# Modulation products in plain float32 on four column strips of the array

## Chip, cores and metric

The kernel runs on one core of a Trainium2 chip. The metric is the device time of one execution in microseconds (us). PE is the tensor engine, DVE the vector engine, ACT the scalar engine, POOL GpSimd and SP the queue that issues most DMAs.

## What is computed

Two layers of a diffusion block on 256 latent and 256 context tokens of width 1024. Each layer begins with a modulation: the conditioning vectors `c` (latent) and `c_ctx` (context) pass a SiLU and are multiplied with a 1024 x 6144 matrix.

```python
s_c, s_cc = silu(c), silu(c_ctx)
mod   = s_c  @ w_ada[l] + b_ada[l]      # 6144 numbers: sh1, sc1, g1, sh2, sc2, g2
mod_c = s_cc @ w_ada[l] + b_ada[l]
y  = mixer_sublayer(x * (1 + sc1) + sh1, ...)       # conv | attention | Hyena | SSD, then w_out
x  = layer_norm(alpha * x + g1 * y)
x  = layer_norm(alpha * x + g2 * peer(x * (1 + sc2) + sh2, ...))   # expert layer, 16384 experts
```

All weights are float32. The result is the latent stream after two layers.

## The kernel before

The modulation is cut into 12 chunks of 512 columns per layer, `c4` = 0 to 11; chunks 0 and 1 are sh1, 2 and 3 sc1, 4 and 5 g1, 6 to 9 sh2 and sc2, 10 and 11 g2. `ada_steps(l, c4, use)` makes one chunk from four loads of `w_ada` of 512 KB each (two halves `j` of 256 columns, two halves `q` of the 1024 rows), here called tiles. A tile holds four blocks of 128 rows, `k` = 0 to 3. The two SiLU vectors are the stationary operand (128 rows, 2 or 4 columns), the weights move through. All eight row blocks of a half accumulate into the same two or four rows of a PSUM bank `pm`.

There are two ways for the product. Where `prep` has a "split" entry, the tile is cut into two `float32r` numbers: ACT casts it to `w_hi` (L140), DVE or POOL subtracts to get `w_lo` (L141), and two products per block (L275, L276) multiply both with `s4`, which holds the vector's own high and low part. Fourteen chunks go that way: the first four of layer 0, five during the expert layer's query stage of layer 0, five in layer 1's mixers. Ten chunks go without: one plain float32 product per block (L278). A plain float32 product leaves two records in the trace, a `float32r` one leaves one.

The finished rows are copied by ACT to `rw` (L284) and then turned into columns. For the first four chunks `to_cols_pe` does it with four small float32 products against a selection matrix (`pt`, L298), the bias being a fifth row. For other chunks below 10 `to_cols` writes the rows to DRAM (`ad`, L303), reads them back element by element, one DMA for each row (`ct`, L307), and DVE adds the bias (L310) and, after a split, the low part (L312). Chunks 10 and 11 are spread with `row_out` (`pg`, L317) and stored as rows.

The program has a start (the first four chunks, then the modulated input `h`, split into `hT`), the mixers' projections (`pj`), a stretch in which the generators `ssd()`, `attention()`, `hyena()`, `conf_norm()` and `more()` take turns, the output projection (`po`), the query stage of the expert layer (`pq`, `ss`, top-k on DVE), the expert tables (`G`, `au`, `ov`), and the same again for layer 1. `more()` and, in the query stage, a call after each query block draw chunks one tile at a time from `modulations()`. A list scheduler orders each engine's instructions by program order and a simulated timeline; the engines run their queues in order. Tiles of `w_ada` are held in rings: six buffers at the start, three (`fwp`) for the rest of layer 0, the four of `w_raw` in layer 1, which the projections use too. A load waits until its ring has a free buffer.

Of the kernel before, what the change touches and what calls it, by code (L numbers as in the profile page):

```python
# [10 lines left out]
F32 = mybir.dt.float32  # L11
F32R = mybir.dt.float32r
# [4 lines left out]
ALU = mybir.AluOpType  # L17
# [21 lines left out]
WRB = (3, 4)  # L39
WLB = (2, 3)  # L40
# [5 lines left out]
WHB = (4, 5)  # L46
FP = ((), (4, 5, 6))
WB = 3
# [6 lines left out]
GRB = (3, 2)  # L55
def AE(G, V): return (G,)
UEV = (0, 0)
AEV = 2
GB = 8
# [27 lines left out]
def tile_hybrid_diffusion(ctx: ExitStack, tc: tile.TileContext, I: dict, out: bass.AP):  # L87
    nc = tc.nc
# [30 lines left out]
    cp = pool("cp")  # L119
# [32 lines left out]
    sT = mk(cp, [128, 8, 2], name="sT")  # L152
    s4 = mk(cp, [128, 8, 4], F32R, name="s4")
    cnt, wdma = [0], [None]
# [98 lines left out]

    def ada_steps(l, c4, use, pe_bias=False):

        pm = bank("pm")
        pr, nb = prep["raw"]
        sp = prep.get("split")
        if sp and c4 in FP[l] and not pe_bias:
            sp = None  # L260
        nr = 4 if sp else 2
        for j in range(2):
            o = pm[0:nr, j * 256:(j + 1) * 256]
            for q in range(2):
                raw = mk(pr, [128, 8, 128], tag=prep.get("tag", "wa_raw"), bufs=nb).rearrange("p (k a) c -> p k (a c)", a=2)
                wdma[0] = nc.sync.dma_start(raw, I["w_ada"][l, 2 * c4 + j, q])
                if sp:
                    hi, lo = (mk(sp[0], [128, 8, 128], F32R, tag=t, bufs=sp[1]) for t in ("w_hi", "w_lo"))
                    hi, lo = (a.rearrange("p (k a) c -> p k (a c)", a=2) for a in (hi, lo))
                    cnt[0] += 1  # L270
                    split(raw, hi, lo, sp[2][cnt[0] % len(sp[2])])
                for k in range(4):
                    st, sp_ = q == 0 and k == 0, q == 1 and k == 3
# [8 lines left out]
        if pe_bias or c4 >= 10:  # L282
            nc.sync.dma_start(rw[nr:nr + 1, :], I["b_ada"][l, c4:c4 + 1, :])
        S.copy(rw[0:nr, :], pm[0:nr, :])  # L284
        use(rw, nr)
        yield
# [7 lines left out]

    def to_cols_pe(rw, nr, l, m0, c):
        pt = bank("pt")
        for j in range(4):
            T.matmul(pt[:, 128 * j:128 * j + 128], rw[0:5, j * 128:(j + 1) * 128], sel[0:5, 0:128], start=True, stop=True)  # L298
        V.tensor_scalar(modTs[l][:, m0:m0 + 4, :], pt.rearrange("p (a b) -> p a b", b=128)[:, :, 0:2], 1.0 if c in SCL else 0.0, None, op0=ALU.add)

    def to_cols(rw, nr, l, m0, c):
        ad = mk(dr, [nr, 512], tag=f"ad{nr}", bufs=2)
        nc.sync.dma_start(ad, rw[0:nr, :])  # L303
        ct = mk(lnp, [128, 4, nr], tag=f"ct{nr}")
        with nc.allow_non_contiguous_dma(reason="a few columns"):
            for r in range(nr):
                nc.sync.dma_start(ct[:, :, r], ad[r].rearrange("(m p) -> p m", p=128))  # L307
        o = modTs[l][:, m0:m0 + 4, :]
        bias = bTs[l][:, 4 * c:4 * c + 4, None].to_broadcast([128, 4, 2])
        V.tensor_tensor(o, ct[:, :, 0:2], bias, ALU.add)  # L310
        if nr == 4:
            V.tensor_tensor(o, o, ct[:, :, 2:4], ALU.add)  # L312

    def row_out(rw, nr, dst, s):
        pg = bank("pg")
        c = (384 if nr == 2 else 128) + s * 128
        T.matmul(pg, sel[0:nr + 1, c:c + 128], rw[0:nr + 1, :], start=True, stop=True)  # L317
        ro = mk(lnp, [1, 512], tag="ro1")
        S.copy(ro, pg[0:1, :])
        nc.sync.dma_start(dst, ro)  # L320
# [517 lines left out]
    MC = {0: 0, 1: 4, 2: 8, 3: 12, 4: 16, 5: 20, 6: 24, 7: 28, 8: 32, 9: 36}  # L838
    SCL = (2, 3, 8, 9)
    g2d = mk(dr, [3, D], name="g2d")  # L840
    xd = mk(dr, [4, 128, D], name="xd")
    prep = {}
    done = [(0, 3)]

    def modulations():

        def g2row(rw, nr, rows, c):
            for s, r in rows:
                row_out(rw, nr, g2d[r:r + 1, (c % 2) * 512:(c % 2) * 512 + 512], s)
        for l, c in [(0, c) for c in range(4, 12)] + [(1, c) for c in range(12)]:  # L850
            def use(rw, nr):
                if c < 10:
                    to_cols(rw, nr, l, MC[c], c)
                else:
                    g2row(rw, nr, ((0, 0), (1, 1)) if l == 0 else ((0, 2),), c)
                done.append((l, c))
            for _ in ada_steps(l, c, use):
                yield (l, c)
# [15 lines left out]
    for l in range(2):  # L874
# [11 lines left out]
        with ExitStack() as mx:  # L886
# [15 lines left out]
            else:  # L902
                with ExitStack() as hs_:
                    hmp = pool("hmp", bufs=2, stack=hs_)
                    prep.update(raw=(hmp, 6), split=(hmp, 3, (V, G)))
                    xt = yT
                    fs_ = pool("fs", stack=fl_s, side="right")

                    def early():
                        nc.sync.dma_start(sel, I["sel"])  # L910
                        nc.sync.dma_start(cm, I["cm"])
                        yield
                        for j in range(2):
                            nc.sync.dma_start(sms[j], I["sm"][j])
                            nc.gpsimd.dma_start(rowss[j], I["rows"][j].partition_broadcast(128))
                        nc.sync.dma_start(dfts[0], I["dft"][:, 0:2])
                        for j in range(2):
                            for _ in hyena_filter(j, fs_, fs_, dfts[0]):
                                yield
                    side = early()  # L920

                    def first():
                        pend = []
                        for i, c4 in enumerate((0, 2, 1, 3)):
                            late = pend
                            pend = []
                            for _ in ada_steps(0, c4, lambda rw, nr: pend.append((rw, nr, 0, MC[c4], c4)), True):
                                for a in late:
                                    to_cols_pe(*a)
                                late = []  # L930
                                yield
                        to_cols_pe(*pend[0])
                    for i, _ in enumerate(first()):
# [14 lines left out]
                prep.update(raw=(fwp, 3))  # L948
                for j in range(2):
                    bT = bTs[j]  # L950
                    nc.sync.dma_start(bT, I["bT"][j])
                    for m0 in (8, 32):
                        V.tensor_scalar(bT[:, m0:m0 + 8], bT[:, m0:m0 + 8], 1.0, None, op0=ALU.add)

# [98 lines left out]
        with ExitStack() as rt:  # L1053
# [395 lines left out]
def _consts():  # L1449
# [18 lines left out]
    put("rot", rot)  # L1468
    s = np.zeros((5, 640), f)
    for r in (0, 2, 4):  # L1470
        s[r, 0:128:2] = 1
        s[r, 128:256] = 1
    for r in (1, 3, 4):
        s[r, 1:128:2] = 1
        s[r, 256:384] = 1
    s[0, 384:512] = 1
    s[1, 512:640] = 1
    s[2, 384:640] = 1
    iE = np.ascontiguousarray(np.broadcast_to(i.astype(np.float16)[None, :, None], (128, 128, TC)))
# [88 lines left out]
```

## Time and profile before

| | us |
|---|---|
| median of 3 runs (lowest to highest) | 3058.21 (3057.75 to 3060.6) |
| the profiled execution, device time | 3056.95 |
| its span, first to last instruction | 3055.2 |
| PE busy | 2787.2 (91%) |
| DVE busy | 2132.8 (70%) |
| ACT busy | 1230.8 (40%) |
| POOL busy | 859.0 (28%) |

Busy time is that of an engine's instructions; overlapping matmuls count once. Device time and span differ by 1.75 us.

### The profile page before, as it was taken

To read this page: it belongs to the slowest core of one execution; us is meant where nothing else is said; L and a number is where in the kernel's file an instruction comes from. 1 tells how busy PE (TensorE), PEld (TensorE's weight loads), DVE (VectorE), ACT (ScalarE), POOL (GpSimd) and SP (SyncE) were. 2 spreads that over 40 slices of the span, in tenths; PEclk is the share of its full clock that TensorE was granted. 3 is DMA by queue.
4 is the path that set the end of the run, shared out by engine and by line. 5 is a ranking of instruction groups with operands and counts; after the bars stand their busy time and mean duration, and the time that the engine had idled before them with its cause. 6 is when DMAs were issued, how large, how long until landed. Compare 5 with 4: busy or idle time off the path is not lost.

```text
span 3055.2 us, 41971 instructions
## 1 busy us (share of the span) xinstructions
PE 2787.2 (91%) x15506; PEld 2388.4 (78%) x15506; DVE 2132.8 (70%) x4278; ACT 1230.8 (40%) x1869; POOL 859.0 (28%) x545
## 2 busy tenths in 40 slices
PE   6798988779999999999999998888779999999997
PEld 4674566549989988888888887666778999999986
DVE  5955448986667777888777646975897675555556
ACT  4233533334533333333333334345444554444443
POOL 4233014623213444454334103442644100000000
PEclk8899989889999999999999999988889999999999
DMA  6123433344598999999989635424435886767656
GB/s 235 56 93 90 134 116 97 111 120 173 213 305 301 314 318 334 319 326 315 313 302 310 229 123 173 128 77 146 138 96 196 276 289 215 213 202 215 204 177 196
DMA packets 266096, 625.23 MB, mean 205 GB/s; under 512 B 46751, under 2 KB 128993, under 8 KB 260258
## 3 DMA queue, kind: packets, MB, share of 16 engines
q1 hardware_dynamic: 225410, 475.20, 47.8%
q0 software_dynamic: 40480, 147.36, 13.6%
q8 instruction: 121, 1.98, 0.3%
q14 instruction: 85, 0.70, 0.1%
HBM read 573.09 MB, written 49.39 MB: 204 GB/s over the span
## 4 chain that ended last, share of the span: by engine, by line
PE 49%; DVE 20%; DMA 13%; issue 10%; POOL 6%; ACT 2%; SPq 0%; POOLq 0%; DVEq 0%; ACTq 0%
DMA grow<-in_vg_dram,eu 8%; PE au L144 5%; PE au L146 5%; PE au L145 5%; PE ov L145 5%; PE ov L144 5%; PE ov L146 5%; POOL grow L1345 5%; PE G L1249 2%; PE G L1250 2%; DVE yT L397 2%; DMA grow<-in_lnr_dram 2%; PE pj L144 1%; DVE e L1101 1%; PE pj L145 1%
## 5 line engine op out<-in xcount | busy, mean ns | idle before, releaser
L146 PE MATMUL au<-hT,u_lo 128*128 128x384 f32 (+1 forms) x2048 | 640.9, 313 | 7.0 <-DVE u_lo L141 3.8
L144 PE MATMUL au<-hT,u_hi 128*128 128x384 f32 (+1 forms) x2048 | 643.6, 314 | 4.1 <-ACT u_hi L140 4.1
L145 PE MATMUL au<-hT,u_hi 128*128 128x384 f32 (+1 forms) x2048 | 640.3, 313 | 0.0
L145 PE MATMUL ov<-v_lo,wh 128*128 128x512 f32 x1280 | 505.8, 395 | 23.1 <-DVE v_lo L141 22.8
L146 PE MATMUL ov<-v_hi,wl 128*128 128x512 f32 x1280 | 501.0, 392 | 0.0
L144 PE MATMUL ov<-v_hi,wh 128*128 128x512 f32 x1280 | 461.4, 394 | 6.7 <-ACT wh L140 6.7
L140 ACT CAST u_hi<-u_raw 128x1024 fp32r<-128x1024 f32 x256 | 268.7, 1050 | 478.4 <-PE au L145 381.4
L144 PEld LDWEIGHTS au<-hT,u_hi 128*128 128x128 f32 x2048 | 393.3, 192 | 13.0 <-ACT u_hi L140 4.8
L146 PEld LDWEIGHTS au<-hT,u_lo 128*128 128x128 f32 x2048 | 392.1, 192 | 10.3 <-DVE u_lo L141 5.7
L145 PEld LDWEIGHTS au<-hT,u_hi 128*128 128x128 f32 x2048 | 392.6, 192 | 8.5 <-issue 0.9
L141 DVE TENSOR_TENSOR v_lo<-v_raw,v_hi 128x1024 fp32r<-128x1024 f32 x255 | 312.8, 1227 | 79.5 <-ACT v_hi L140 79.3
L141 DVE TENSOR_TENSOR u_lo<-u_raw,u_hi 128x1024 fp32r<-128x1024 f32 x198 | 242.1, 1223 | 155.5 <-ACT u_hi L140 155.5
L140 ACT CAST v_hi<-v_raw 128x1024 fp32r<-128x1024 f32 x256 | 268.1, 1048 | 100.4 <-DMA v_raw<-in_v_dram 82.7
L140 ACT CAST wh<-act 128x384 fp32r<-128x384 f32 (+1 forms) x256 | 117.3, 461 | 469.5 <-PE ov L145 469.3
L145 PEld LDWEIGHTS ov<-v_lo,wh 128*128 128x128 f32 x1280 | 242.4, 189 | 78.0 <-DVE v_lo L141 34.1
L144 PEld LDWEIGHTS ov<-v_hi,wh 128*128 128x128 f32 x1280 | 242.5, 190 | 51.9 <-ACT wh L140 7.0
L146 PEld LDWEIGHTS ov<-v_hi,wl 128*128 128x128 f32 x1280 | 242.2, 189 | 50.1
L141 POOL TENSOR_TENSOR w_lo<-w_raw,w_hi 128x1024 fp32r<-128x1024 f32 (+1 forms) x85 | 207.9, 2451 | 228.7 <-ACT w_hi L140 200.1
L1345 POOL DMA_INDIRECT grow<-in_ug_dram,eu x128 | 163.4, 1277 | 270.3 <-DVE grow L1349 228.5
L1345 POOL DMA_INDIRECT grow<-in_vg_dram,eu x128 | 173.7, 1357 | 216.8 <-DVE accg L1358 175.4
L141 POOL TENSOR_TENSOR u_lo<-u_raw,u_hi 128x1024 fp32r<-128x1024 f32 x58 | 150.4, 2600 | 266.7 <-ACT u_hi L140 186.9
L1358 DVE SCALAR_TENSOR_TENSOR accg<-grow,ag,accg 128x1024 f32<-128x1024 f32 x127 | 162.9, 1283 | 78.9 <-DMA grow<-in_vg_dram,eu 78.2
(838 smaller groups left out, 4834.7 us busy)
## 6 DMA issues: line engine op xcount, KB each, us to landing
u_raw<-in_uT_dram SPq DMA_DIRECT2D x256, 512.0 KB, 4.7
v_raw<-in_v_dram SPq DMA_DIRECT2D x256, 512.0 KB, 4.4
Gd<-stg SPq DMA_DIRECT2D x40, 1024.0 KB, 4.8
gt<-Gd SPq DMA_DIRECT2D x80, 512.0 KB, 7.3
wa_raw<-in_w_ada_dram SPq DMA_DIRECT2D x76, 512.0 KB, 3.6
w_raw<-in_w_in_t_dram SPq DMA_DIRECT2D x44, 512.0 KB, 3.6
w_raw<-in_wq_dram SPq DMA_DIRECT2D x32, 512.0 KB, 3.6
w_raw<-in_w_ada_dram SPq DMA_DIRECT2D x20, 512.0 KB, 4.3
```

What stands on the lines that cost most here:

```text
L140: S.copy(hi, src)
L141: late["V" if eng in (None, V) else "G"] = (eng or V).tensor_tensor(lo, src, hi.bitcast(F32), ALU.subtract)
L144: T.matmul(o, lh, rh, start=first, stop=False)
L145: T.matmul(o, lh, rl, start=False, stop=False)
L146: return T.matmul(o, ll, rh, start=False, stop=last)
L397: V.scalar_tensor_tensor(uc, upad[:, m, :, j:j + 256], wj, uc, op0=ALU.mult, op1=ALU.add)
L1101: V.tensor_tensor(x[:, :, :, 0:w], x[:, :, :, 0:w], x[:, :, :, w:2 * w], ALU.add)
L1249: T.matmul(b[:, j * 128:(j + 1) * 128], B_[:, tt // TC, :, tt % TC], Ah[:, tt // TC, :, tt % TC], start=True, stop=False)
L1250: T.matmul(b[:, j * 128:(j + 1) * 128], B_[:, tt // TC, :, tt % TC], Al[:, tt // TC, :, tt % TC], start=False, stop=True)
L1345: nc.gpsimd.indirect_dma_start(out=r, out_offset=None, in_=I[tab], in_offset=bass.IndirectOffsetOnAxis(ap=eu[:, i:i + 1], axis=0))
L1358: V.scalar_tensor_tensor(accg, r, ag[:, i:i + 1], accg, op0=ALU.mult, op1=ALU.add)
```

## The change

The products of the modulation are no longer split. The stationary operand becomes `s32`, the two SiLU vectors followed by 30 columns of zeros. Row block `k` of a tile writes its own 32 PSUM partitions, 32k to 32k+31, so that the four blocks of a tile lie on four strips of 32 array columns; each strip accumulates over `q`. ACT copies all 128 partitions to `rw`. The rows become columns by four products with a selection matrix of 128 rows, which also sums the strips; DVE adds the bias from `bTs`. `to_cols` by way of DRAM is gone. `row_out` uses the same selection, and its bias comes by a second product. The ring of `w_ada` tiles at the start has nine buffers instead of six and two of three. The loads of `bTs` and the four small additions to them move to the start of the program.

```diff
-    sel = mk(cp, [5, 640], name="sel")
+    sel = mk(cp, [128, 3, 128], name="sel")
...
-    s4 = mk(cp, [128, 8, 4], F32R, name="s4")
+    s32 = mk(cp, [128, 8, 32], name="s32")
+    G.memset(s32, 0.0)
     sig(sT, craw)
-    V.tensor_tensor(sT, sT, craw, ALU.mult)
-    S.copy(s4[:, :, 0:2], sT)
-    V.tensor_tensor(s4[:, :, 2:4], sT, s4[:, :, 0:2].bitcast(F32), ALU.subtract)
+    V.tensor_tensor(s32[:, :, 0:2], sT, craw, ALU.mult)
...
         for j in range(2):
-            o = pm[0:nr, j * 256:(j + 1) * 256]
             for q in range(2):
                 raw = mk(pr, [128, 8, 128], ...)
                 wdma[0] = nc.sync.dma_start(raw, I["w_ada"][l, 2 * c4 + j, q])
-                if sp:
-                    hi, lo = (mk(sp[0], [128, 8, 128], F32R, tag=t, bufs=sp[1]) for t in ("w_hi", "w_lo"))
-                    split(raw, hi, lo, sp[2][cnt[0] % len(sp[2])])
                 for k in range(4):
-                    if sp:
-                        T.matmul(o, s4[:, 4 * q + k, :], hi[:, k, :], start=st, stop=False)
-                        T.matmul(o, s4[:, 4 * q + k, :], lo[:, k, :], start=False, stop=sp_)
-                    else:
-                        T.matmul(o, sT[:, 4 * q + k, :], raw[:, k, :], start=st, stop=sp_)
+                    T.matmul(pm[32 * k:32 * k + 32, j * 256:(j + 1) * 256], s32[:, 4 * q + k, :], raw[:, k, :], start=q == 0, stop=q == 1)
...
-        rw = mk(lnp, [5, 512], tag="rw")
-        S.copy(rw[0:nr, :], pm[0:nr, :])
+        rw = mk(lnp, [128, 512], tag="rw")
+        S.copy(rw, pm)
...
-    def to_cols(rw, nr, l, m0, c):
-        ad = mk(dr, [nr, 512], tag=f"ad{nr}", bufs=2)
-        nc.sync.dma_start(ad, rw[0:nr, :])
-            for r in range(nr):
-                nc.sync.dma_start(ct[:, :, r], ad[r].rearrange("(m p) -> p m", p=128))
+    def to_cols(rw, l, m0, c):
         pt = bank("pt")
         for j in range(4):
+            T.matmul(pt[:, 128 * j:128 * j + 128], rw[:, j * 128:(j + 1) * 128], sel[:, 0, :], start=True, stop=True)
+        V.tensor_tensor(modTs[l][:, m0:m0 + 4, :], pt.rearrange("p (a b) -> p a b", b=128)[:, :, 0:2],
+                        bTs[l][:, 4 * c:4 * c + 4, None].to_broadcast([128, 4, 2]), ALU.add)
...
-        T.matmul(pg, sel[0:nr + 1, c:c + 128], rw[0:nr + 1, :], start=True, stop=True)
+        T.matmul(pg, sel[:, 1 + s, :], rw, start=True, stop=False)
+        T.matmul(pg, cst["ones"][0:1, :], br, start=False, stop=True)
...
-                    prep.update(raw=(hmp, 6), split=(hmp, 3, (V, G)))
+                    prep.update(raw=(hmp, 9))
...
                         nc.sync.dma_start(sel, I["sel"])
+                        for j in range(2):
+                            nc.sync.dma_start(bTs[j], I["bT"][j])
+                            for m0 in (8, 32):
+                                V.tensor_scalar(bTs[j][:, m0:m0 + 8], bTs[j][:, m0:m0 + 8], 1.0, None, op0=ALU.add)
...
-                prep.update(raw=(wp, WRB[1]), tag="w_raw", split=(wp, WLB[1], ((G,), (V,), (G, G, V), (G, V))[AEV]))
+                prep.update(raw=(wp, WRB[1]), tag="w_raw")
...
-                if l == 0:
-                    prep.update(split=(wp, WB, AE(G, V)))
-                else:
+                if l:
```

## Rows read from the trace of the kernel before

**Rows 1.** Stretches: length, PE, PEld, DVE, ACT, POOL busy, clock, DMA share, GB/s.

```profile
0.00:58.00 58.00, 34.71 (x169) 19.20 (x170) 34.35 (x51) 28.89 (x36) 27.21 (x19) 0.90 0.84 289
58.00:236.00 178.00, 158.46 (x679) 121.71 (x680) 132.30 (x189) 55.99 (x87) 62.10 (x36) 0.93 0.23 74
236.00:369.00 133.00, 120.56 (x576) 60.95 (x574) 65.85 (x169) 56.79 (x118) 19.36 (x24) 0.94 0.41 123
...
424.00:470.00 46.00, 32.51 (x137) 25.17 (x135) 20.48 (x62) 22.77 (x40) 13.67 (x8) 0.78 0.45 162
470.00:690.00 220.00, 174.47 (x838) 127.11 (x836) 204.91 (x919) 76.99 (x98) 101.98 (x38) 0.88 0.37 109
690.00:1870.00 1180.00, 1143.86 (x5982) 1036.62 (x5980) 837.54 (x1233) 427.41 (x609) 391.63 (x293) 0.99 0.81 277
...
1975.00:2106.00 131.00, 106.45 (x600) 74.30 (x599) 99.56 (x182) 65.90 (x119) 56.66 (x33) 0.89 0.39 123
```

**Rows 2.** Chain that ended last, 0 to 75 us: start, length, what.

```profile
30.02 2.88 POOL w_lo L141
...
37.03 7.48 DMA yT<-in_xT_dram
44.53 6.07 DMA w_raw<-in_w_in_t_dram
...
57.72 0.80 PE pj L144
```

**Rows 3.** Chain, 236 to 369 us: shares by line, then pieces.

```profile
by line: PE pm L278 25.1%; PE yi L587 6.8%; PE py L764 6.7%; DMA ad<-rw 4.7%; PE uf L560 4.0%; PE ptr L755 3.4%; DMA ct<-ad 3.4%; PE sg L643 3.0%; POOL am L642 2.9%; PE yo L680 2.6%; PE ea L670 2.4%; PE sc L739 2.3%; ACT L600 1.9%; ACT L603
...
247.13 3.63 DMA ad<-rw
...
251.21 2.23 DMA ct<-ad
```

**Rows 4.** Chain pieces with the records of one group of products each.

```profile
301.55 0.59 PE yd L658 x8
...
317.94 1.82 PE pm L278 x8
319.76 0.81 PE ea L670 x12
...
336.34 3.54 PE pm L278 x16
...
459.09 0.89 PE ss L1084 x8
459.98 1.91 PE pg L317 x4
```

**Rows 5.** Chain around the end of layer 0's output projection.

```profile
417.24 4.41 PE pm L278 x20
...
423.39 6.26 DMA w_raw<-in_wq_dram
```

**Rows 6.** Query stage: a stretched DVE line, min/median/max, and POOL beside it.

```profile
L1155 DVE TENSOR_TENSOR e<-e,dec x8: 733/1026/3535, 519.5 to 2274.7; 128x1024 f16<-128x1024 f16 x4, 128x512 f16<-128x512 f16 x4
...
577.35 3.52 DVE L1155 TENSOR_TENSOR e<-e,dec 128x1024 f16<-128x1024 f16 x1
...
579.63 3.27 POOL L141 TENSOR_TENSOR w_lo<-wa_raw,w_hi 128x1024 fp32r<-128x1024 f32 x1
...
L141 POOL TENSOR_TENSOR w_lo<-wa_raw,w_hi x20: 2360/2418/3869, 456.6 to 626.3; 128x1024 fp32r<-128x1024 f32 x20
```

**Rows 7.** Layer 1's mixers, 1975 to 2106 us: chain by line, a piece.

```profile
by line: issue 8.4%; ACT w_hi L140 5.4%; PE py L764 5.1%; DVE w_lo L141 4.8%; PE pj L144 4.4%; PE pj L145 4.4%; PE pj L146 3.9%; POOL w_lo L141 3.8%; DVE dt L483 3.7%; PE pm L275 3.2%; PE pm L276 3.2%; PE yi L587 2.9%; PE pg L317 2.9%; PE p
...
2085.98 2.35 POOL w_lo L141
```

**Rows 8.** PE idle until ACT's copy `rw`, us and times: `pg`, then `pt`.

```profile
  ACT rw L284: 14.4, 6
...
  ACT rw L284: 4.6, 4
```

More of the change, by code (lines that the diff above doesn't have):

```diff
@@ L46 @@
 WHB = (4, 5)
-FP = ((), (4, 5, 6))
 WB = 3
@@ L55 @@
 GRB = (3, 2)
-def AE(G, V): return (G,)
 UEV = (0, 0)
-AEV = 2
 GB = 8
@@ L152, in tile_hybrid_diffusion @@
     sT = mk(cp, [128, 8, 2], name="sT")
-    s4 = mk(cp, [128, 8, 4], F32R, name="s4")
-    cnt, wdma = [0], [None]
+    s32 = mk(cp, [128, 8, 32], name="s32")
+    wdma = [None]
+    G.memset(s32, 0.0)
     sig(sT, craw)
-    V.tensor_tensor(sT, sT, craw, ALU.mult)
-    S.copy(s4[:, :, 0:2], sT)
-    V.tensor_tensor(s4[:, :, 2:4], sT, s4[:, :, 0:2].bitcast(F32), ALU.subtract)
+    V.tensor_tensor(s32[:, :, 0:2], sT, craw, ALU.mult)
     smp = pool("smp")
@@ L251, in load_w, with ada_steps @@
         return hi, lo
-    def ada_steps(l, c4, use, pe_bias=False):
+    def ada_steps(l, c4, use):
         pm = bank("pm")
         pr, nb = prep["raw"]
[L258 to L261, printed above, removed]
         for j in range(2):
-            o = pm[0:nr, j * 256:(j + 1) * 256]
             for q in range(2):
@@ L266, in ada_steps @@
                 wdma[0] = nc.sync.dma_start(raw, I["w_ada"][l, 2 * c4 + j, q])
-                if sp:
-                    hi, lo = (mk(sp[0], [128, 8, 128], F32R, tag=t, bufs=sp[1]) for t in ("w_hi", "w_lo"))
-                    hi, lo = (a.rearrange("p (k a) c -> p k (a c)", a=2) for a in (hi, lo))
-                    cnt[0] += 1
-                    split(raw, hi, lo, sp[2][cnt[0] % len(sp[2])])
-                for k in range(4):
-                    st, sp_ = q == 0 and k == 0, q == 1 and k == 3
-                    if sp:
-                        T.matmul(o, s4[:, 4 * q + k, :], hi[:, k, :], start=st, stop=False)
-                        T.matmul(o, s4[:, 4 * q + k, :], lo[:, k, :], start=False, stop=sp_)
-                    else:
-                        T.matmul(o, sT[:, 4 * q + k, :], raw[:, k, :], start=st, stop=sp_)
+                for k in range(4):
+                    T.matmul(pm[32 * k:32 * k + 32, j * 256:(j + 1) * 256], s32[:, 4 * q + k, :], raw[:, k, :], start=q == 0, stop=q == 1)
                 if j * q == 0:
                     yield
-        rw = mk(lnp, [5, 512], tag="rw")
-        if pe_bias or c4 >= 10:
-            nc.sync.dma_start(rw[nr:nr + 1, :], I["b_ada"][l, c4:c4 + 1, :])
-        S.copy(rw[0:nr, :], pm[0:nr, :])
-        use(rw, nr)
+        rw = mk(lnp, [128, 512], tag="rw")
+        S.copy(rw, pm)
+        use(rw)
         yield
@@ L293, in run, with row_out @@
                     gens.remove(g)
-    def to_cols_pe(rw, nr, l, m0, c):
+    def to_cols(rw, l, m0, c):
         pt = bank("pt")
         for j in range(4):
-            T.matmul(pt[:, 128 * j:128 * j + 128], rw[0:5, j * 128:(j + 1) * 128], sel[0:5, 0:128], start=True, stop=True)
-        V.tensor_scalar(modTs[l][:, m0:m0 + 4, :], pt.rearrange("p (a b) -> p a b", b=128)[:, :, 0:2], 1.0 if c in SCL else 0.0, None, op0=ALU.add)
-    def to_cols(rw, nr, l, m0, c):
-        ad = mk(dr, [nr, 512], tag=f"ad{nr}", bufs=2)
-        nc.sync.dma_start(ad, rw[0:nr, :])
-        ct = mk(lnp, [128, 4, nr], tag=f"ct{nr}")
-        with nc.allow_non_contiguous_dma(reason="a few columns"):
-            for r in range(nr):
-                nc.sync.dma_start(ct[:, :, r], ad[r].rearrange("(m p) -> p m", p=128))
[L308 to L314, printed above, removed]
+            T.matmul(pt[:, 128 * j:128 * j + 128], rw[:, j * 128:(j + 1) * 128], sel[:, 0, :], start=True, stop=True)
+        V.tensor_tensor(modTs[l][:, m0:m0 + 4, :], pt.rearrange("p (a b) -> p a b", b=128)[:, :, 0:2],
+                        bTs[l][:, 4 * c:4 * c + 4, None].to_broadcast([128, 4, 2]), ALU.add)
+    def row_out(rw, br, dst, s):
         pg = bank("pg")
-        c = (384 if nr == 2 else 128) + s * 128
-        T.matmul(pg, sel[0:nr + 1, c:c + 128], rw[0:nr + 1, :], start=True, stop=True)
-        ro = mk(lnp, [1, 512], tag="ro1")
+        T.matmul(pg, sel[:, 1 + s, :], rw, start=True, stop=False)
+        T.matmul(pg, cst["ones"][0:1, :], br, start=False, stop=True)
+        ro = mk(lnp, [1, 512], tag="ro1", bufs=1)
         S.copy(ro, pg[0:1, :])
@@ L845, in modulations, with g2row, use @@
     def modulations():
-        def g2row(rw, nr, rows, c):
+        def g2row(rw, l, rows, c):
+            br = mk(lnp, [1, 512], tag="br1", bufs=1)
+            nc.sync.dma_start(br, I["b_ada"][l, c:c + 1, :])
             for s, r in rows:
-                row_out(rw, nr, g2d[r:r + 1, (c % 2) * 512:(c % 2) * 512 + 512], s)
+                row_out(rw, br, g2d[r:r + 1, (c % 2) * 512:(c % 2) * 512 + 512], s)
         for l, c in [(0, c) for c in range(4, 12)] + [(1, c) for c in range(12)]:
-            def use(rw, nr):
+            def use(rw):
                 if c < 10:
-                    to_cols(rw, nr, l, MC[c], c)
+                    to_cols(rw, l, MC[c], c)
                 else:
-                    g2row(rw, nr, ((0, 0), (1, 1)) if l == 0 else ((0, 2),), c)
+                    g2row(rw, l, ((0, 0), (1, 1)) if l == 0 else ((0, 2),), c)
                 done.append((l, c))
@@ L926, in first @@
                             pend = []
-                            for _ in ada_steps(0, c4, lambda rw, nr: pend.append((rw, nr, 0, MC[c4], c4)), True):
+                            for _ in ada_steps(0, c4, lambda rw: pend.append((rw, 0, MC[c4], c4))):
                                 for a in late:
-                                    to_cols_pe(*a)
+                                    to_cols(*a)
                                 late = []
                                 yield
-                        to_cols_pe(*pend[0])
+                        to_cols(*pend[0])
                     for i, _ in enumerate(first()):
@@ L948, in tile_hybrid_diffusion @@
                 prep.update(raw=(fwp, 3))
[L949 to L953, printed above, removed]
             def more():
@@ L1468, in _consts @@
     put("rot", rot)
[L1469 to L1478, printed above, removed]
+    s = np.zeros((128, 3, 128), f)
+    s[0::32, 0, 0::2] = 1
+    s[1::32, 0, 1::2] = 1
+    s[0::32, 1] = 1
+    s[1::32, 2] = 1
     iE = np.ascontiguousarray(np.broadcast_to(i.astype(np.float16)[None, :, None], (128, 128, TC)))
```

1 line of the change is left out of this document (removed).

## Prediction

> **What bounds the kernel now.** I read the busy times by stretch first [rows 1]. In 690 to 1870 us, the expert tables of layer 0, PE is busy 1144 of 1180 us; that stretch and its counterpart in layer 1 hold two thirds of the span, and the change touches neither. It can only pay in the stretches that hold modulation chunks, and each of them has another limit.
>
> The start, 0 to 58 us, has the DMA engines busy 0.84 of the time and no compute engine over 0.6 [rows 1]. The chain there [rows 2] runs through splits (`w_lo`), then through the load of `xT`, which is issued behind the last tile of `w_ada`, then through `w_raw`, and the projections flow from 57.7 us.
>
> From 236 to 369 us PE is busy 121 of 133 us [rows 1], and the chain of waits [rows 3] gives 25.1% of this stretch to the plain products `pm`, 33.4 us. Another 8.1%, 10.8 us, is the way through DRAM (`ad`, then `ct`): DVE stands before its bias addition until the scattered columns land.
>
> From 470 to 690 us DVE is the limit, 205 of 220 us [rows 1]. Part of that is not work. A DVE line that takes 1.03 us in the median takes 3.52 us where POOL's `w_lo` runs beside it [rows 6]. In 1975 to 2106 us no engine is full (PE 106, DVE 100 of 131) [rows 1], and the chain passes from splits to `pm` and back [rows 7].
>
> **The change, part by part.**
>
> *Price of one tile.* A block of 8 records takes 1.82 us on the chain, one of 16 takes 3.54 [rows 4]: 0.215 us a record and 0.10 us fixed for each block. The trace holds no product on four strips, but it has two on two: `ea` and `yd` put their outputs on the two halves of the partitions. `ss`, on the full width, takes 0.89 us for 8 records of 128 columns, 0.11 each; `ea` takes 0.81 us for 12 and `yd` 0.59 us for 8 [rows 4]. Without 0.16 us fixed that is 0.054 each: two halves run abreast, in `yd` with different moving data. Four abreast make 2 x 0.215 + 0.10 = 0.53 us a tile, two abreast 0.96, none 1.82. I take four, since the step from one to two was a full factor, and keep the others for the range.
>
> [...]
>
> *Start (A).* Sixteen ACT casts and sixteen `w_lo` go. Nine buffers that free after the products instead of after a split let SP issue all loads, `xT` among them, without waiting for POOL. The bytes stay: 58 us at 0.84 share are 49 us at full share [rows 1], so at most 9 us. `h` and its splits keep DVE and POOL after `xT` has landed. I take -7, bounds -10 and +3 (below, first rival). `s32`'s memset, the four `bTs` additions and SP's two loads ahead of `cm` cost nothing while the first tile is on its way; without that cover they would add about 1.5 us of small instructions and issue.
>
> *Mixers of layer 0 (B).* On the chain stand 33.4 / 1.82 = 18.3 tiles; at 0.53 they leave 9.7, -23.7. Six conversions come to PE, each four products of 128 columns, 8 records like `ss`: 0.89 + 0.10, +5.9 in all, as the stretch is PE's. Of the 10.8 us through DRAM I count only -3: ACT's copy, the four products and DVE follow one another in its place, and with DVE 66 and ACT 57 of 133 us busy, attention's softmax steps are late next. SP loses the waits of `ct` on `ad`, so the loads queued behind move up; three buffers are enough at one tile in four us. Sum -21, bounds -30 and +3.
>
> *End of the output projection (C).* 20 records of `pm` in 4.41 us, 4 more just after, and the first query weight, queued on SP behind a `w_ada` load that waits for these products, lands 6.26 us later [rows 5]. 24 records become three tiles, 1.6 us: -4, bounds -8 and 0.
>
> *Query stage (D).* Twenty POOL splits of 2.42 us and twenty ACT casts go, POOL 102 to 54 us. Below, nothing: if the stretched DVE lines sit beside the remaining splits. Above, each split stretches DVE by its whole length, 48 us, cut at about 27 where PE's 174 of 220 us becomes the limit. The row nearest is L1155: a median of 1.03 against a maximum of 3.54 says that fewer than half of its instructions are caught [rows 6]. I take three tenths, -14. PE's own change (tiles cheaper, seven conversions more) is covered by its 45 idle us; were it not, it would cost those 7 us.
>
> *Layer 1's mixers (E).* `w_lo` on DVE and POOL and `pm` are 4.8 + 3.8 + 3.2 + 3.2% of 131 us, 19.7 us, and DVE's stretches beside 13 splits come on top; some `w_lo` are the projections' own. Back come 20 tiles, 10.6 us of PE, mostly beside other work, three conversions, and two `row_out` with one more product each of about 1 us (`pg`, two products in 1.91 us [rows 4]). I take -11, bounds -21 and 0.
>
> The sum: -7 - 21 - 4 - 14 - 11 = -57. The profiled execution took 3056.95 us, which is 1.3 below the median of the runs: 3056.95 - 57 = 3000 us, and that is the forecast. What follows a stage waits for its last result, so gains of successive stages add up; nothing between them takes a fixed time from the start of the program.
>
> **The rivals.**
>
> *The strips don't run abreast.* Then the change doesn't do what it says. For it: two halves are no proof for four, each with its own stream. [...] A: 16 tiles take 29 to 58 us, about +3. B: 0 + 5.9 - 3 = +3. C: 0. D: PE gets 17 us more (20 tiles x (1.82 - 0.96), a split tile being 8 records of half the length), mostly covered, -10. E: the same 17 us on a PE with 25 idle, -5. Sum -9: 3048 us.
>
> *The next engine takes what PE and POOL give.* In B, DVE's and ACT's softmax chain; in D, PE waits for ACT's `qs` and DVE's top-k stays in order; in E, attention, which no split delays. For it: PE's 12 idle us in B already end at DVE and ACT results. Against: none of these is busy over 0.55 in B [rows 1]. Half of the gain stays: 3028 us.
>
> *PE stands in its queue behind ACT's copy: slower.* Each conversion now makes PE wait for `rw`, and all products queued behind it wait too. `pg` already idles PE for 14.4 us in six waits, `pt` for 4.6 in four [rows 8]: 2.4 and 1.2 us. There are 16 new conversions. At 2.4 us they cost 38 us, and the forecast falls to 19 us of gain; it turns at 57 / 16 = 3.6 us each. With 4 us each, ACT's queue being fuller in the mixers, +7: 3064 us. Against: beside the generators PE has other products that the scheduler can put between.
>
> [...]
>
> **How the numbers follow.** The forecast with its sizes gets 0.62 (its own range 2975 to 3025: the bounds of A to E don't all fall on one side), strips not abreast 0.10, gain halved 0.16, PE behind ACT 0.07, clock 0.05. The range for 8 in 10 cuts the last 0.07 and part of the first rival at the top and the sum of the better bounds (2965) at the bottom: 2970 to 3042. A measurement of this kernel tells about 0.2%, 6 us, from no change. Faster takes the forecast, the halved gain, the clock and most of the first rival, 0.89; same, what of the first and third lies between 3052 and 3064, 0.05; slower 0.06.
>
> **What the profile of the changed kernel would show.** Eight `pm` records of one tile within about 0.53 us, their starts in fours; in threes or pairs, 0.96; in a row, the first rival. `xT` landing near 38 us instead of 44.5, and projections from about 50. `pm` at some 8% of the chain between start of the generators and `po`, no `ad` and `ct`, that stretch 21 us shorter. L1155's maximum still near 3.5 us but fewer stretched instructions, the query stage 14 us shorter. PE's idle time before `pt` well under 2 us each. The prediction would be wrong if the stretch after 470 us kept its 220 us with DVE less busy, if `pt` idled PE over 3 us each, or if a reordered queue left PE waiting elsewhere, above all in 58 to 236 us, where no modulation is made and nothing should change.

## The result and the profile after

The changed kernel takes 2986.15 us (median of 4 runs, 2981.73 to 2991.8), the kernel before 3059.4 in the same session (3057.75 to 3066.09): a ratio of 0.9758, 95% interval 0.9735 to 0.978. That is 73 us less, where 57 were forecast; 3000 us were forecast and 2986 came. The profiled execution took 2991.8 us, with a span of 2990.0.

To see where the time went I cut every span at the same products of PE (the first `pj`, the last `pj`, the first `po` and so on; `tr` and `G` are products behind the query blocks, `ov` the expert tables). Lengths in us; each labelled run is told below.

| stretch | before | after | one strip | conversion alone | GpSimd work back |
|---|---|---|---|---|---|
| start to first `pj` (A) | 51.7 | 44.8 | 47.6 | 52.1 | 44.5 |
| `pj` of layer 0 | 176.9 | 172.2 | 173.0 | 176.6 | 172.8 |
| mixers of layer 0, to `po` (B) | 140.5 | 129.7 | 146.7 | 147.0 | 129.8 |
| end of `po` to `pq` (C) | 30.0 | 28.8 | 30.1 | 30.1 | 31.9 |
| query stage, `pq` to `tr` (D) | 223.9 | 201.1 | 220.3 | 241.2 | 225.6 |
| `G` to `ov` | 184.6 | 177.8 | 177.6 | 176.6 | 177.7 |
| `ov` of layer 0 | 994.9 | 1005.4 | 994.5 | 993.0 | 993.3 |
| mixers of layer 1, to `po` (E) | 99.2 | 81.4 | 101.3 | 107.4 | 85.2 |
| whole span | 3055.2 | 2990.0 | 3042.5 | 3074.6 | 3027.7 |

Two rows of it are not the change's. The `ov` stretch lies between 993 and 1005 us in all fourteen traces of this study, in no order that follows an edit; the changed kernel's own profile has a long one. PE is busy in it for 969 us before and 971 after, and what makes it longer or shorter was not separated. `G` to `ov` is near 178 or near 184 us, and takes the longer value in four of the later variants too. From the first `po` of layer 1 to the end, which the table leaves out, the span took 949 us before, 942 after and 945 to 948 in the other twelve traces; no modulation is made there.

Stretches of the changed kernel, as in [rows 1]: length, then busy time of PE, PEld, DVE, ACT and POOL, granted clock, DMA share, GB/s.

```profile
0.00:51.00 51.00, 25.79 (x175) 11.85 (x176) 20.01 (x43) 13.43 (x20) 10.57 (x13) 0.90 0.92 334
...
225.00:347.00 122.00, 99.18 (x625) 57.78 (x624) 66.08 (x169) 54.13 (x114) 18.34 (x23) 0.92 0.39 130
...
448.00:644.00 196.00, 158.30 (x897) 121.54 (x890) 181.91 (x917) 58.45 (x77) 49.25 (x18) 0.89 0.38 122
...
1935.00:2048.00 113.00, 96.56 (x623) 65.43 (x622) 68.77 (x167) 48.62 (x99) 24.67 (x20) 0.94 0.39 132
```

The start now keeps its DMA engines at 0.92 and 334 GB/s instead of 0.84 and 289. POOL's busy time in the query stage is half of what it was [rows 1]. In layer 0's mixers PE is busy 99 of 122 us, no longer 121 of 133: it has stopped being the bound there.

The chain of the start, as in [rows 2]:

```profile
18.12 10.46 DMA wa_raw<-in_w_ada_dram
28.59 7.30 DMA yT<-in_xT_dram
...
44.76 0.79 PE pj L141
```

No split stands in it before `xT` any more. `xT` lands at 35.9 us instead of 44.5, and the projections begin 7 us earlier. One more piece is gone. Before, the last of the additions to `bTs` stood on the chain between the loads and `h`, and the change moved them to the start of the program:

```profile
50.59 2.09 DVE bT L953 x3
```

The chain of layer 0's mixers, as in [rows 3] and [rows 4]: shares by line, then two pieces with their records.

```profile
by line: PE py L732 11.1%; PE yi L555 7.2%; PE pm L260 6.4%; PE ptr L723 5.7%; PE pt L278 4.3%; PE uf L528 4.3%; PE sg L611 3.5%; PE sc L702 3.5%; PE sc L707 3.3%; PE yo L648 2.8%; ACT hT L713 2.7%; DVE t2k L618 2.7%; PE ea L638 2.6%; PE yd
...
277.36 1.00 PE pm L260 x16
...
287.55 0.89 PE pt L278 x8
```

`pm` fell from 25.1% to 6.4%, `ad` and `ct` are gone, and the conversion `pt` has come in with 4.3%, at the 0.89 us that was taken from `ss`. A single tile stands as one piece in a narrower view of the chain; the second line is the view of the products on `pm`, the duration of one record as min/median/max:

```profile
291.80 0.57 PE pm L260 x8
```

```profile
L260 PE MATMUL pm<-wa_raw,s x8: 379/391/403, 291.7 to 292.0; 128*32 128x256 f32 x8
```

Eight records that each last 0.39 us fit into 0.57 us. In the trace they start in fours, 6 to 7 ns apart, and the second four 0.24 us after the first: all four strips run abreast, as the prediction took it (0.53).

### The profile page after: what moved, and what is told of

Its sections match the earlier page's. It is cut to its first block, busy times and chain, and to the rows that moved or that the text cites. A ratio compares the mean times of both kernels' runs of the same rounds, so it can differ in the third digit from the quotient of the medians.

```text
span 2990.0 us, 41926 instructions
## 1 busy us (share of the span) xinstructions
PE 2721.2 (91%) x15646; PEld 2352.7 (79%) x15646; DVE 2058.4 (69%) x4255; ACT 1179.0 (39%) x1810; POOL 754.3 (25%) x505
## 4 chain that ended last, share of the span: by engine, by line
PE 53%; DVE 17%; DMA 13%; issue 9%; POOL 5%; ACT 2%; SPq 0%; POOLq 0%; DVEq 0%; ACTq 0%
DMA grow<-in_vg_dram,eu 9%; PE ov L141 6%; PE ov L142 6%; PE ov L143 6%; PE au L141 5%; PE au L143 5%; PE au L142 5%; POOL grow L1311 4%; PE G L1215 3%; PE G L1216 3%; DVE yT L365 2%; PE pj L141 1%; DVE accg L1324 1%; PE pj L142 1%; PE pj L143 1%
## 5 line engine op out<-in xcount | busy, mean ns | idle before, releaser
L138 POOL TENSOR_TENSOR w_lo<-w_raw,w_hi 128x1024 fp32r<-128x1024 f32 (+1 forms) x72 | 177.8, 2478 | 252.7 <-ACT w_hi L137 221.8
```

Source lines behind the costliest of these rows:

```text
L138: late["V" if eng in (None, V) else "G"] = (eng or V).tensor_tensor(lo, src, hi.bitcast(F32), ALU.subtract)
```

## The experiments

### How much is the strips: one, two or four of them

One strip: all four blocks of a tile go to it in turn, and the row is read from 32 partitions. Two strips: the same with `k % 2`. Everything else is as changed.

```
-T.matmul(pm[32 * k:32 * k + 32, ...], ..., start=q == 0, stop=q == 1)
+T.matmul(pm[0:32, ...], ..., start=q == 0 and k == 0, stop=q == 1 and k == 3)
```

> The changed kernel with all four row blocks of a tile on the first strip of 32 columns, accumulating one after the other; loads, rings, conversions by matmul and the absence of splits stay. Theory (the four strips run abreast and that is what makes a plain float32 tile cheap): a tile's block of 8 records goes from 0.57 us back to about 1.82 us, 76 + 20 tiles, 120 us more of PE, of which the start gives back 8 to 15 us, layer 0's mixers 8 to 18, layer 1's mixers 5 to 12, the query stage 0 to 10 (DVE is the limit there): 21 to 45 us slower than the changed kernel, still faster than before. Rival (the gain comes from the splits and the way through DRAM that are gone, the strips add nothing that PE's idle time would not have held): at most 8 us slower than the changed kernel.

> The changed kernel with the four blocks of a tile on two strips of the array, two blocks one after the other on each: same products, same records, half the concurrency. A tile should take 0.96 us instead of 0.57. If the time follows the length of a tile (theory), one third of what a single strip cost comes back: about 18 us slower than the change, near 3004 us, with the query stage of layer 0 and the mixers of both layers 5 to 7 us longer each. If the other engines cover tiles up to about 1 us and only the longer ones show (rival), the loss is under 6 us.

One strip: 3044.58 us, ratio 0.9949 (0.993 to 0.9969), 58 us more than the change. Two strips: 3004.42 us, 0.9814 (0.9784 to 0.9844), 18 us more. A tile on one strip in the chain of layer 0's mixers, the chain of layer 1's mixers there, and the changed kernel's tile and one on two strips in the timeline:

```profile
297.86 1.84 PE pm L260 x8
```

```profile
by line: PE pm L260 38.5%; PE py L732 7.8%; PE ptr L723 4.5%; PE sc L702 4.2%; PE sc L703 3.8%; PE yi L555 3.8%; PE sg L611 3.5%; PE pt L278 3.3%; PE uf L528 2.8%; PE ea L638 2.3%; PE pg L284 2.2%; PE st L585 2.2%; PE yo L648 2.1%; ACT rw L
```

```profile
291.73 0.64 PE L260 MATMUL pm<-wa_raw,s 128*32 128x256 f32 x8
287.68 1.06 PE L260 MATMUL pm<-wa_raw,s 128*32 128x256 f32 x8
```

The loss follows the length of a tile: 1.27 us more cost 58 us, about 0.4 us more cost 18. The place does so only in part: with two strips the start loses 2.8 us, the mixers 6.1 and 2.4, but the query stage nothing (198.8). And the run with one strip is itself the change without its strips: splits gone, conversion by matmul, no DRAM. Of the 73 us that leaves some 14, at the start and in the `pj` behind it (4 us each), in the query stage (4) and in `G` to `ov`, whose 7 are not the change's; both mixers are longer than before the change.

This must not be read as the strips' own worth where splits went. A split tile was two `float32r` products per block, eight records with a median of 0.28 us each before, and a plain tile leaves eight of 0.38; on one strip PE is busy 95.8 us in layer 1's mixers, where it was 76.3 before. Layer 1's mixers before, on one strip, on two, and with the change:

```profile
2006.70:2105.80 99.10, 76.32 (x435) 48.61 (x433) 74.60 (x139) 56.01 (x100) 38.88 (x24) 0.86 0.37 113
1994.00:2095.30 101.30, 95.75 (x464) 54.27 (x463) 48.67 (x130) 39.95 (x81) 9.87 (x12) 0.92 0.36 116
1970.10:2054.30 84.20, 76.67 (x466) 44.94 (x464) 48.26 (x129) 39.01 (x80) 9.26 (x12) 0.93 0.41 137
1966.20:2047.70 81.50, 66.22 (x465) 39.18 (x463) 49.16 (x130) 40.69 (x82) 9.83 (x12) 0.94 0.43 141
```

On two strips PE is busy as long as before (77 and 76 us), and the stage is 15 us shorter than before: most of its gain comes with the splits that are gone, as long as the plain products cost PE no more than the split ones. What part the granted clock, 0.93 against 0.86, had in it was not separated.

### The conversion alone

The kernel before, with its splits and its one strip; only the way through DRAM is replaced by four matmuls.

```
-nc.sync.dma_start(ad, rw[0:nr, :]) ... ct ... V.tensor_tensor(o, ct[:, :, 0:2], bias, ALU.add)
+T.matmul(pt[:, 128 * j:128 * j + 128], rw[0:nr, ...], sel[0:nr, 0:128], ...)
+V.tensor_tensor(modTs[l][:, m0:m0 + 4, :], pt..., bias, ALU.add)
```

> The kernel before with one part of the change alone: rows become columns by four products and one DVE addition also for chunks 4 and up, nothing goes through DRAM; splits and plain products stay as before. Theory (the way through DRAM held DVE and SP up in layer 0's mixers): 3 to 11 us less in the stretch between the last projections and the output projection, a little less in the query stage, since SP no longer waits for the rows there; 3 to 12 us faster than before. Rival (that wait was hidden beside PE's products, and 16 conversions of 1 us on a full PE cost what they give): from 2 us faster to 6 us slower than before.

3071.77 us, ratio 1.0035 (1.0019 to 1.0052): 11 to 13 us slower than before. Both theories were too kind. PE's waits in the query stage (line, waited for: us in total, times, longest):

```profile
PE pt L304 <- ACT rw L284: 18.1, 7, 9.8
PE pm L275 <- ACT w_hi L140: 12.2, 1, 12.2
PE hb L829 <- DVE h L823: 10.6, 1, 10.6
PE pq L144 <- ACT w_hi L140: 10.3, 2, 6.8
```

This fits the third rival's mechanism: PE stands at `pt` until ACT has copied the row, 2.6 us each time, with all else queued behind it. The query stage got 17 us longer, and the mixer stages 6.5 and 8.2. The 10.8 us through DRAM in [rows 3] brought nothing back: in layer 0's mixers PE's busy time grew by as much as the stretch, from 127.2 to 133.6 us.

### What the splits cost in the query stage

Three runs of the changed kernel put one of the two halves of a split back as idle work, at each tile of layer 0's query stage and of layer 1's mixers: on GpSimd (`G, G, V` in turn in layer 1), the same reading constants, so that no weight buffer is held, and ACT's copy. They write a scratch tile of float16, where the splits wrote four bytes for each number.

```
 wdma[0] = nc.sync.dma_start(raw, I["w_ada"][l, 2 * c4 + j, q])
+de[dcnt[0] % len(de)].tensor_tensor(dt_, raw, raw, ALU.subtract)      # GpSimd
+de[dcnt[0] % len(de)].tensor_tensor(dt_, cmd_, cmd_, ALU.subtract)    # on constants
+S.copy(dt_, raw)                                                      # ACT
```

> The changed kernel with a subtraction of each modulation tile from itself put back, 128 x 1024 float32 into a scratch tile that nobody reads: on POOL for the 32 tiles of the query stage of layer 0, on POOL, POOL and DVE in turn for the 20 tiles of layer 1's mixers. Theory (POOL's splits stretched DVE instructions beside them, and that was the largest part of the gain in both stages): the query stage 15 to 30 us longer, layer 1's mixers 5 to 13 us, 20 to 40 us slower than the changed kernel in all. Rival (the gain there came from PE, ACT and the shared rings of split tiles): at most 6 us slower.

> The changed kernel with the same extra subtractions on GpSimd as in the run before that added them, at the same places, but reading a table of constants in place of the weight tile, so that no weight buffer is held until the subtraction ends. That run lost 42 us, 24.5 of them in the query stage of layer 0, with 29 subtractions there of 2.1 us each. Theory 1: GpSimd's work itself costs, as it stretches VectorE's lines and delays the splits behind it; then the query stage again becomes 20 to 25 us longer than the change's and the whole ends near 3026 us. Theory 2: the cost was the weight buffer held longer, that is, later loads; then the query stage stays within 6 us of the change and the whole below 3000 us.

> The same with a copy on ACT of each of these tiles (128 x 1024 float32 into a scratch tile) in place of the subtraction. Theory (ACT's casts were covered): 0 to 5 us slower than the changed kernel. Rival (ACT stood in the way of the query results and of attention): 10 us or more slower.

ACT's copies: 2992.32 us (0.9761 to 0.9807), 6 us more than the change, with intervals that overlap; layer 1's mixers took 6 us longer (87.6, at a granted clock of 0.85 against 0.94), the query stage did not (197.5). GpSimd's subtractions: 3028.11 us (0.9874 to 0.9926), 42 more, the query stage back at 225.6. On constants: 3032.71 us (0.9868 to 0.9936), query stage 217.5. There, loosed from the loads, the subtractions of layer 1 ran early and crowded its `pj` (125.5 us instead of 113.6), so that total tells nothing of the question, but the query stage does: 16 of 24 us come back with no buffer held, and DVE is busy 189.6 us there. That the rest is the weight buffer is not shown: 26 of the subtractions fall into the stage instead of 29, and the stage itself takes 195.0 us in the run without chunks 4 to 9 and 199.7 with the ring of six, against the change's 201.1.

The query stage before, with the change, on one strip, on two strips, and with GpSimd's work put back, cut at `pq` and `tr`, columns as above:

```profile
446.10:670.00 223.90, 178.38 (x826) 125.60 (x827) 198.18 (x938) 78.13 (x100) 98.91 (x37) 0.88 0.36 106
```

```profile
422.80:623.90 201.10, 163.40 (x891) 119.77 (x892) 171.48 (x934) 59.53 (x80) 45.42 (x17) 0.89 0.37 117
```

```profile
444.50:664.80 220.30, 202.79 (x890) 140.05 (x891) 172.22 (x944) 58.91 (x78) 41.01 (x16) 0.92 0.31 104
```

```profile
434.00:632.80 198.80, 176.17 (x890) 125.30 (x891) 166.20 (x935) 57.36 (x77) 37.99 (x16) 0.92 0.35 114
```

```profile
426.40:652.00 225.60, 167.59 (x890) 121.98 (x891) 199.31 (x936) 58.95 (x78) 101.87 (x45) 0.85 0.31 101
```

With GpSimd's work DVE is back at 199 of 226 us, where it was before the change (198 of 224), and the gain is gone. With one strip PE becomes the bound (203 of 220), but it has 24 us more to do there than before the change. Two strips tell the two apart: PE is busy 176 us, as before (178), and the stage keeps its whole gain. So it is DVE's relief that shortens this stage, and of PE it asks only that it take on little more than it had. DVE's instructions are nearly the same in all five: 27 to 28 us of its time come and go with 53 to 56 us of GpSimd's.

### What bounds the mixers of layer 0

Chunks 4 to 9 of layer 0 are left out.

```
+if l == 0 and 4 <= c4 <= 9:
+    for _ in range(3): yield
+    V.tensor_copy(modTs[l][:, 4 * c4:4 * c4 + 4, :], bTs[l][...].to_broadcast([128, 4, 2]))
+    done.append((l, c4)); yield; return
```

> The changed kernel without the modulation of chunks 4 to 9 of layer 0: their loads, products, copies and conversions are left out and their columns take the bias alone. The question is what bounds the mixers of layer 0 (129.7 us from the last pj to the first po with the change, 140.5 before it). Theory 1: the gain was smaller than predicted because the attention tail and VectorE set the pace there once the products had shrunk; then leaving the products out altogether takes at most 6 us more off that stretch (123 to 130 us). Theory 2: the tiles and their loads still set the pace; then the 18 tiles that fall there, at 0.57 us each, and five conversions at 1.2 us give back 16 us or more (114 us or less).

125.4 us in its one run (2981.29 us in all), within the first theory's range of 123 to 130. The stretch, PE's longest wait in it, and one group of products on its chain:

```profile
222.30:347.70 125.40, 93.44 (x423) 57.27 (x421) 71.06 (x178) 56.90 (x121) 21.78 (x28) 0.81 0.08 29
```

```profile
PE yd L633 <- DVE t2k L628: 19.0, 4, 10.0
```

```profile
260.03 1.12 PE yd L633 x8
```

Without any modulation PE waits 19 us for DVE's `t2k`, which feeds `yd`. The stretch before and with the change, PE's waits that grew (the first line is of before), and the same products on the chain:

```profile
228.60:369.10 140.50, 127.19 (x614) 65.17 (x612) 72.24 (x187) 60.92 (x127) 23.09 (x28) 0.94 0.40 121
217.00:346.70 129.70, 106.12 (x662) 61.67 (x661) 72.41 (x187) 58.45 (x125) 22.14 (x28) 0.92 0.38 126
```

```profile
PE yd L658 <- DVE t2k L653: 6.6, 2, 3.3
PE yd L626 <- DVE t2k L621: 12.0, 4, 4.4
PE pt L278 <- ACT rw L264: 4.3, 3, 2.9
PE pm L260 <- DMA wa_raw<-in_w_ada_dram: 2.2, 1, 2.2
```

```profile
268.71 0.66 PE yd L626 x8
```

PE lost 21.1 us of work by the change, and the stretch only 10.8: PE's idle time rose from 13.3 to 23.6 us, at `t2k` (5.4 us more), at the new conversion (4.3) and at one load (2.2). That much is shown without the run that leaves the chunks out.

That run takes 4.3 us off the change, but this is not yet the price of the modulation, for its granted clock is 0.81 against 0.92. All four groups of `yd` on its chain take 1.12 us; with the change three of four take 0.66. The changed kernel's products there less `pm` (16.6 us) and `pt` (6.7) are 83 us of PE; here they took 93. As an estimate from these numbers, at the change's clock the stretch could be up to 10 us shorter, and the modulation costs between 4 and 15 us there. The second theory (114 us or less) isn't excluded. The start of this run also took 49.0 us to the first `pj`, as 19 loads of `w_ada` stand ahead of `xT` in it, not 16: that time goes with the order of the loads.

### The ring at the start

`raw=(hmp, 6)` in place of `raw=(hmp, 9)`.

> The changed kernel with a ring of six weight buffers at the start, as before the change, in place of nine. Theory: the loads are free of stops because the tiles are read by products alone and a product frees its buffer within a microsecond or two of the landing; then the ring's length hardly matters, and the first projection comes within 2 us of the change's 44.8 us. Rival: the three buffers more are what lets the loads, xT among them, be queued without a stop; then the start falls back by 5 to 7 us, towards the 51.7 us before the change. Elsewhere nothing changes.

2982.69 us (0.9719 to 0.9778), the first `pj` at 44.9 us. The three buffers more do nothing. What is left to free the loads is that a tile is read by products alone; with these on one strip the first `pj` comes at 47.6.

### A later conversion, and more draws

The conversion one draw later (with one draw added behind chunks that something waits for); two draws of modulation after each query block; both; and the later conversion with the ring of six.

```
 S.copy(rw, pm)
-use(rw)
 yield
+use(rw)
...
-if done[-1] < (1, (FL, 11)[l]): next(fill)
+for _ in range(2 - l):
+    if done[-1] < (1, (FL, 11)[l]): next(fill)
```

> The changed kernel with the conversion of a finished row set one draw later, so that matrix work of the surrounding stage stands between ScalarE's copy of the row and the product that reads it. With the change TensorE waits 40.8 us in 27 places for that copy. Theory: the waits lie on the path in the mixers of layer 1 and in the query stage of layer 0 (10.6 us in 7 there), and 8 to 15 us of them come back: 2971 to 2978 us. Rival: other limits (loads, VectorE) end at the same place, and less than 4 us comes back; or the draw that is added pushes the last tiles later, up to 5 us slower.

> The changed kernel with two draws of modulation work after each query block of layer 0 instead of one, so that fewer tiles are left for the end of that stage, where they follow one another at the pace of their loads (TensorE waits 11.0 us in 7 for loads there). Theory: the end of the query stage loses those waits, 5 to 15 us faster (2971 to 2981 us). Rival: the tiles' splits on GpSimd and VectorE crowd the query blocks instead and what is saved at the end is lost before: within 4 us of the change.

> Both the later conversion (2977.3 us alone, 9 us faster than the change) and two draws per query block in layer 0 (2992.5 us alone, no gain; TensorE waited 30 us in 12 places for ScalarE's copy there). Theory: two draws brought nothing because each brought twice the waits for the copy; with the conversion one draw later they are gone, and the query stage ends 4 to 8 us earlier than with the later conversion alone (191.0 us): 2969 to 2974 us. Rival: the stage is bound by VectorE and GpSimd as well, the draws only move work, and the whole stays within 3 us of 2977 us or gets slower.

> The later conversion (2977.3 us, interval of its ratio 0.9692 to 0.9753, which overlaps that of the change, 0.9735 to 0.9780) together with the ring of six buffers at the start, which alone moved nothing (2982.7 us). Open is whether the later conversion gains at all: its waits for ScalarE's copy in the query stage did not become fewer (13.3 us in 6 against 10.6 in 7), though that stage was 191.0 us against 201.1. Theory: the conversion's place is worth 8 to 10 us in that stage; then it takes 189 to 194 us here too and the ratio lies below 0.9735. Rival: the stage varies by that much with how the engines happen to meet (195 to 204 us in the runs that left it unchanged); then it comes out anywhere in that range and the ratio near 0.975.

The 40.8 us in 27 of the first expectation count PE's weight loads beside its products; of products alone it is 16.6 us in 13 places. The times: 2977.32 us (0.9692 to 0.9753), 2992.47 (0.9738 to 0.9795), 2983.96 (0.9705 to 0.9761) and 2983.06 (0.9734 to 0.9772). The later conversion shortens the query stage in both of its runs with one draw, to 191.0 and 190.0 us, but not by the waits that I named: `pt` still idles PE 13.3 us in 6 places in the first of them, against the change's 10.6 in 7 (the run comes first):

```profile
PE pt L278 <- ACT rw L264: 13.3, 6, 6.6
PE pm L260 <- DMA wa_raw<-in_w_ada_dram: 7.7, 4, 2.2
PE tr L1177 <- DVE sl L1136: 4.0, 1, 4.0
PE ss L1052 <- ACT qs L1046: 2.2, 1, 2.2
```

```profile
PE pm L260 <- DMA wa_raw<-in_w_ada_dram: 11.0, 7, 3.0
PE pt L278 <- ACT rw L264: 10.6, 7, 6.0
PE ss L1050 <- ACT qs L1044: 9.0, 1, 9.0
PE tr L1175 <- DVE sl L1134: 5.8, 1, 5.8
```

It is `qs` (9.0 to 2.2) and the loads that are waited for less. Both runs then have the longer `G` to `ov` (183.5 and 183.6 us), and the second lost 5 us in layer 0's mixers, so over the whole kernel a gain isn't established: the last interval is that of the change. Two draws gained nothing either way.

The lost 5 us go with the clock. Layer 0's mixers with the later conversion, then with the ring of six beside it:

```profile
217.30:347.30 130.00, 107.37 (x662) 62.89 (x660) 72.06 (x187) 60.77 (x127) 22.04 (x28) 0.91 0.37 126
216.50:351.70 135.20, 113.44 (x663) 67.21 (x661) 72.06 (x187) 61.02 (x127) 23.76 (x28) 0.86 0.37 125
```

The same products took PE 6 us longer at a granted clock of 0.86. Both together, late conversion and two draws, show the same there (135.1 us, 0.86).

## Why the prediction came out as it did

**Direction and main mechanism: right.** Four strips run abreast at 0.57 us a tile against a forecast 0.53, and with one strip 58 of the 73 us are lost. The reading behind "a full factor" was off: with the same 0.16 us taken off, `ss` takes 0.09 us a record, and the step from one to two abreast was 1.7, not 2. The first rival, at 3048 us, came near what the kernel on one strip does (3044.6), but its terms didn't: it had the start 3 us longer and the query stage 10 us shorter than before, and they came 4 and 4 us shorter. Of its 29 to 58 us for the sixteen tiles of the start no run shows the upper end: on one strip the first two tiles on the chain took 6.34 us there, later ones 1.75 each (46 records in 10.05 us, 32 in 7.02).

**Start (A): right in size, -6.9 against -7; half of its reason fell.** Nine buffers were named for it, and six do as well. Another 4.7 us came where nothing was forecast, in `pj` of layer 0; one strip has most of it (173.0), the conversion alone, which keeps the splits, has not (176.6). The additions to `bTs`, which the prediction looked at only as a cost (with the change four of 0.17 us each, and 0.92 us of SP for their two loads), fit: 2.09 us of them stood on the chain at the first `pj`, and in the conversion alone they stay there. Which part of the new start shortens `pj` was not tested alone.

**Mixers of layer 0 (B): -10.8 against -21, the step that failed.** Its prices held (`pm` 0.57, `pt` 0.89), and PE's work fell by the 21 us of the sum. Wrong was taking all of PE's saved time as time that would go: half of it became idle. The second rival's mechanism, held against by "none of these is busy over 0.55", is what happened: DVE, busy 72 of 130 us, makes PE wait 12.0 us for `t2k` where it waited 6.6, and the conversion and a load add 6.5. The share of an engine's busy time said nothing about a chain of dependent steps. The six conversions less the way through DRAM were summed at +2.9; put in alone they cost 6.5 us there.

**End of the output projection (C): -1.2 against -4.** Within its bounds; the first query weight still takes 5.75 us to land.

**Query stage (D): -22.8 against -14; the mechanism right, a row misread.** In [rows 6] the median of 1026 mixes two shapes. Of the wide one alone, before and after, with the four instructions of the stage (busy, mean ns):

```profile
L1155 DVE TENSOR_TENSOR e<-e,dec 128x1024 f16<-128x1024 f16 x4 | 11.9, 2973 | 0.0
```

```profile
L1121 DVE TENSOR_TENSOR e<-e,dec 128x1024 f16<-128x1024 f16 x4 | 5.5, 1368 | 0.0
```

Of the four wide ones three took 3.5 us, each with 2.3 us of one GpSimd subtraction beside it, and one, with none, 1.31. So three of the four in this stage were caught, where three tenths were taken. (In two of the three that subtraction is `u_lo`, a split of the expert tables; the `w_lo` shown in [rows 6] came behind it.) DVE lost 27 us of busy time (198.2 to 171.5), not 14, near the upper bound of the term. That PE's own change is covered by its idle time held: with two strips PE is busy as before, and the stage is as short as with four (198.8 us).

**Layer 1's mixers (E): -17.8 against -11, the term mis-sized.** 19.7 us of splits and `pm` were read off the chain and lowered, as PE's work was thought to lie beside other work. With two strips, where PE is busy as before, 15 of the 17.8 us are there: they go with the splits (DVE busy 74.6 to 48.3 us, POOL 38.9 to 9.3), with the clock's part not separated. The two further strips add 3.

**PE behind ACT's copy: the mechanism is there, at a third of the price that decides.** PE waits 16.6 us in 13 places at `pt`, 1.3 us each, where 3.6 would have eaten the gain. Put into the kernel before, it makes it slower. The waits of [rows 8] were also counted with the weight loads; of products alone they are 6.8 us in 3 and 2.0 in 2.

**The clock**, given 0.05 in the chances, fell from 0.94 to 0.92 in layer 0's mixers, not to the 0.78 of the stretch from 424 to 470 us before the change [rows 1], and with PE at 93 of 125 us and no modulation to 0.81. Where it was granted 0.86 with the same products, the stretch was 5 us longer.

**The sum.** B and C fell short by 10 and 3 us; D, E and the `pj` stretch brought 9, 7 and 5 more: 64 us by the stretches against 57. That the sum came nearer than its terms is luck: their errors have both signs. The profiled span shrank by 65 us and the median by 73, since that profile caught a long `ov` stretch and lies 5.7 us above its median, and the profile before lies 2.5 below its own.

## What to carry to other kernels

Time that one engine saves is not yet time that the stretch loses: in layer 0's mixers PE saved 21.1 us and the stretch lost 10.8, with DVE, busy 72 of 130 us, waited for next. The next chain may stand a few microseconds behind, on engines that look half idle, so follow what PE would wait for next. Leaving a piece of work out altogether did not show its price here, as the granted clock was 0.81 without it and 0.92 with it. An experiment that undoes one part can load another engine more than it was loaded before (one strip: PE 203 us in the query stage, 178 before), and then shows more than that part's worth; a half step, here two strips (176 us), that leaves that engine as it was tells the two apart. A change of three parts can hold one that loses: here the conversion by matmul is 11 to 13 us slower by itself and is paid for by the rest.

## What the hardware showed beyond expectation

Four plain-float32 products on four strips, each with its own moving data, overlap nearly in full: two tiles in 1.00 us where one strip took 3.54 [rows 4], 3.5 times. In the query stage 53 to 56 us of GpSimd's float32 subtractions lengthen the same DVE instructions by 27 to 28 us; before the change a wide float16 product took 3.5 us beside one of them and 1.31 without. Copies of the same tiles on ACT leave the stage as it is (197.5 us, against the change's 201.1). The same products of layer 0's mixers took PE 107 us at a granted clock of 0.91 and 113 at 0.86.
